# Residual stream by token tiles: normalise first, then transpose to channels

## The chip, the cores and the metric

The kernel runs on one core of a Trainium2 chip. The metric is device time of one launch in microseconds (us). The kernel before was timed three times: 2730.47, 2731.25 and 2731.49 us, median 2731.25 us. A difference of 0.2% is about 5.5 us.

## The reference

A decoder trunk of two layers over 512 tokens with 1024 channels, all in float32. A layer is three stages, and each adds its normalised result to the residual stream h:

```
f = swiglu(rms_norm(h, ffn1_pre_g), w_gate, w_up, w_down);  h = h + 0.5 * rms_norm(f, ffn1_post_g)
u = rms_norm(h, mix_pre_g);  p = u @ w_in                   # split into four branches and four gates
...
merged = g0 * y_a + g1 * y_b + g2 * y_c + g3 * y_d;         h = h + rms_norm(merged @ w_o, mix_post_g)
f = swiglu(rms_norm(h, ffn2_pre_g), w_gate, w_up, w_down);  h = h + 0.5 * rms_norm(f, ffn2_post_g)
```

`rms_norm(x, g) = x * rsqrt(mean(x * x) + 1e-6) * g`, with the mean over the 1024 channels of a token. `swiglu` has an inner width of 2816. The branches of the mixer are a gated convolution of width 3, a gated convolution of width 31 with a LayerNorm, a differential attention of 4 heads and a forgetting attention of 8 heads. The branch gates are sigmoids of 4096 further columns of `u @ w_in`.

## The kernel before, in words

**Layout.** The stream is held transposed: eight tiles `h` of 128 channels x 512 tokens. All products are taken in split float32: each factor is a high part (rounded by ScalarE in `hi_of`, L148) and a low part (the rest, by VectorE in `lo_of`, L141), and a product is three matmuls, high x high, high x low, low x high (`mm3`, L129 to L131). A stage's inputs are the eight pairs `xh`, `xl`.

**Weights.** They come as one stream of chunks of 128x1024 (512 KB), eight 128x128 blocks each, in the order in which `block` (L103) asks for them. `load` (L90) issues the DMA on SyncE's queue, rounds the high part on ScalarE (L99) and takes the low part on VectorE (L100). There are three raw buffers and five pairs of split ones, and chunks are asked for three ahead (`AHEAD`). So every 24 full-width matmuls cost ScalarE one 128x1024 cast and VectorE one 128x1024 subtraction, everywhere in the program.

**Order.** A scheduler puts the instructions of the program into one fixed queue for each engine when the kernel is built; each engine then works its queue off in order and waits at the head. PSUM has eight tiles of 128x512.

**A boundary** (`boundary`, L208) is what lies between two stages: there are seven of them, one at the start, five between stages and one at the end. The stage's input is h times a gain per channel, not yet normalised; the normalisation, a number for each token, is applied after the next stage's first products, where every result is multiplied by `rb`, a 128x512 tile that holds the 512 factors in every row (L346, L352, L409 to L415, L430 to L440, L477, L490, L558). It is made from sums of squares over channels: ScalarE squares, VectorE adds, TensorE sums over the partitions (`colsum`, L164), VectorE and GpSimdE take the power -1/2 (`rstd`, L172, L173), VectorE makes diagonal tiles (L180), TensorE spreads them (`spread`, L187). The post-norm of the stage behind is made in the same way.

So that TensorE keeps working meanwhile, the last one (FFN) or three (mixer) of the eight column groups of the down projection, and the first four products of the next stage (`outer`, L226), are taken in halves of 256 tokens: while the second half is multiplied, the norm of the first is made, and `update` (L277) goes channel tile by channel tile: multiply, add to h, scale and split, so that the first tile is there early. `CUT` tells after how many products the pieces stand.

## Time and profile before

| | |
|---|---|
| median of three runs | 2731.25 us |
| the profiled execution: its own time, its span | 2730.53 us, 2728.8 us |
| TensorE busy, matmul records | 2706.4 us (99%), 13196 |
| VectorE busy | 1617.6 us (59%) |
| ScalarE busy | 1016.6 us (37%) |
| GpSimdE busy | 55.5 us (2%) |
| DMA | 254.75 MB, mean 93 GB/s |

All times within the program are microseconds from the start of the span. Two matmuls that follow each other overlap in their records, so what a matmul costs is read from the distance of two starts, and a group's "mean ns of one" is longer than that. With VectorE and ScalarE two records overlap by some 0.08 us when the second waits for nothing (two VectorE operations of 0.42 us in 0.75 us).

### The profile page before, as it was taken

What the parts mean: (1) busy time and instruction counts of PE and PEld (TensorE: products, weight loads), DVE (VectorE), ACT (ScalarE), POOL (GpSimd) and SP (SyncE); (2) the same over time, 40 slices, a digit from 0 to 9 for tenths busy, and PEclk for the clock granted to TensorE, in tenths of its full rate; (3) what the DMA queues carried; (4) which work ended last, traced back from release to release, by engine and by line L of the source; (5) the groups of instructions that cost most, each with busy time, mean ns of one, the idle gap of its engine ahead of it and who ended that gap; (6) DMA issues with size and microseconds to landing.
All of it is one profiled execution on the core that took longest, in us unless ns stands there. A gap on an engine that the chain in (4) does not pass through costs nothing.

```text
span 2728.8 us, 33159 instructions
## 1 busy us (share of the span) xinstructions
PE 2706.4 (99%) x13196; PEld 2280.8 (84%) x13196; DVE 1617.6 (59%) x2703; ACT 1016.6 (37%) x1569; POOL 55.5 (2%) x84
## 2 busy tenths in 40 slices
PE   8999999999999999999999999999999999999998
PEld 7888898888888898888888888988888888988887
DVE  6443259988786565443364432699887865654423
ACT  4232242454553343322342322424545533432321
POOL 0000000000000000000000000000000000000000
PEclk9999999999999999999999999999999999999999
DMA  4222222222222222222222222222222222222221
GB/s 171 100 93 100 94 92 95 86 71 85 96 87 89 93 93 93 101 96 98 85 101 95 99 100 93 87 101 84 71 86 93 85 93 93 91 95 98 95 101 54
DMA packets 73786, 254.75 MB, mean 93 GB/s; under 512 B 8464, under 2 KB 10896, under 8 KB 73632
## 3 DMA queue, kind: packets, MB, share of 16 engines
q1 hardware_dynamic: 69264, 246.45, 26.4%
q10 hardware_dynamic: 4368, 6.20, 0.8%
q8 instruction: 103, 1.69, 0.3%
q14 instruction: 51, 0.42, 0.0%
HBM read 250.48 MB, written 2.13 MB: 93 GB/s over the span
## 4 chain that ended last, share of the span: by engine, by line
PE 96%; DVE 3%; ACT 1%; issue 0%; DMA 0%; POOLq 0%; DVEq 0%; ACTq 0%
PE p L129 26%; PE p L130 26%; PE p L131 26%; PE pf L130 2%; PE pf L129 2%; PE pf L131 2%; PE o L548 1%; PE pl L129 1%; PE pl L131 1%; PE pl L130 1%; PE pv L454 1%; PE pv L455 1%; PE pv L453 1%; PE pt L532 1%; PE st L187 1%; PE sc L502 1%
## 5 line engine op out<-in xcount | busy, mean ns | idle before, releaser
L99 ACT CAST wh<-raw 128x1024 fp32r<-128x1024 f32 (+1 forms) x465 | 488.5, 1051 | 1244.7 <-PE p L130 839.9
L129 PE MATMUL p<-xh,wh 128*128 128x512 f32 x2304 | 903.3, 392 | 0.0
L131 PE MATMUL p<-xh,wl 128*128 128x512 f32 x2304 | 897.5, 390 | 0.0
L130 PE MATMUL p<-xl,wh 128*128 128x512 f32 x2304 | 896.7, 389 | 0.0
L100 DVE TENSOR_TENSOR wl<-raw,wh 128x1024 fp32r<-128x1024 f32 (+1 forms) x465 | 566.9, 1220 | 390.3 <-ACT wh L99 389.6
L131 PEld LDWEIGHTS p<-xh,wl 128*128 128x128 f32 x2304 | 432.4, 188 | 91.2
L130 PEld LDWEIGHTS p<-xl,wh 128*128 128x128 f32 x2304 | 432.8, 188 | 88.4 <-issue 0.5
L129 PEld LDWEIGHTS p<-xh,wh 128*128 128x128 f32 x2304 | 432.8, 188 | 88.0 <-PE pt L532 0.5
L129 PE MATMUL p<-gh,wh 128*128 128x512 f32 x616 | 239.6, 389 | 0.0
L130 PE MATMUL p<-gl,wh 128*128 128x512 f32 x616 | 239.6, 389 | 0.0
L131 PE MATMUL p<-gh,wl 128*128 128x512 f32 x616 | 239.6, 389 | 0.0
L352 DVE TENSOR_TENSOR s<-p,rb 128x512 f32<-128x512 f32 x80 | 55.3, 691 | 238.6 <-PE p L131 238.6
L383 DVE SCALAR_TENSOR_TENSOR yc<-ba,vec,yc 128x489 f32<-128x489 f32 (+18 forms) x240 | 171.8, 729 | 1.8
L346 DVE TENSOR_TENSOR s<-p,rb 128x512 f32<-128x512 f32 x80 | 55.3, 691 | 152.6 <-PE p L131 152.5
L129 PEld LDWEIGHTS p<-gh,wh 128*128 128x128 f32 x616 | 115.6, 188 | 24.0
L131 PEld LDWEIGHTS p<-gh,wl 128*128 128x128 f32 x616 | 115.6, 188 | 24.0
L130 PEld LDWEIGHTS p<-gl,wh 128*128 128x128 f32 x616 | 115.6, 188 | 24.0
L129 PE MATMUL pf<-xh,wh 128*128 128x256 f32 (+1 forms) x352 | 104.5, 297 | 6.8 <-ACT wh L99 6.8
L130 PE MATMUL pf<-xl,wh 128*128 128x256 f32 (+1 forms) x352 | 104.3, 296 | 0.0
L131 PE MATMUL pf<-xh,wl 128*128 128x256 f32 (+1 forms) x352 | 103.8, 295 | 0.0
L522 ACT ACTIVATE e<-e,mx 128x128 f32<-128x128 f32 (+3 forms) x128 | 71.2, 557 | 53.8 <-DVE mx L520 42.6
L558 DVE TENSOR_TENSOR s<-p,rb 128x512 f32<-128x512 f32 x64 | 44.1, 689 | 66.8 <-PE p L131 66.7
(206 smaller groups left out, 3228.4 us busy)
## 6 DMA issues: line engine op xcount, KB each, us to landing
raw<-ws SPq DMA_DIRECT2D x463, 512.0 KB, 3.3
cb<-cum ACTq DMA_DIRECT2D x16, 256.0 KB, 3.6
h<-xT SPq DMA_DIRECT2D x8, 256.0 KB, 5.2
outT<-h SPq DMA_DIRECT2D x8, 128.0 KB, 1.7
outT<-h ACTq DMA_DIRECT2D x8, 128.0 KB, 1.7
raw<-ws SPq DMA_DIRECT2D x2, 256.0 KB, 4.4
cst<-consts ACTq DMA_DIRECT2D x1, 384.0 KB
s<-lamv ACTq DMA_DIRECT2D x2, 128.0 KB, 2.1
```

Source lines behind the costliest of these rows:

```text
L99: S.copy(out=wh[:, j], in_=raw[:, j])
L100: V.tensor_sub(out=wl[:, j], in0=raw[:, j], in1=wh[:, j].bitcast(F32))
L129: PE.matmul(out=out, lhsT=w[0], rhs=x[0], start=first, stop=False)
L130: PE.matmul(out=out, lhsT=w[0], rhs=x[1], start=False, stop=False)
L131: PE.matmul(out=out, lhsT=w[1], rhs=x[0], start=False, stop=last)
L187: PE.matmul(out=out[:, i * P:(i + 1) * P], lhsT=ones, rhs=dg[:, i * P:(i + 1) * P], start=True, stop=True)
L346: V.tensor_mul(out=x, in0=pg, in1=rb)
L352: V.tensor_mul(out=u, in0=pu, in1=rb)
L383: V.scalar_tensor_tensor(out=acc[:, s:], in0=y[:, :T - s], scalar=vcol(wname, l, i * 4 + j), in1=acc[:, s:], op0=ALU.mult, op1=ALU.add)
L453: PE.matmul(out=pv[t], lhsT=xh, rhs=wh, start=k == 0, stop=False)
L522: S.activation(out=e, in_=e, func=AF.Exp, scale=-1.0, bias=mx, accum_out=sums)
L558: V.tensor_mul(out=g, in0=p, in1=rb)
```

## The change: what it does

- The stream is held by tokens: four token tiles `hs[t]` of 128 tokens in two halves of 512 channels, read from `x` and written to `out` without a transposition on the host.
- The down projection (and `w_o`) is taken by token tiles (`by_tokens`): the stage's result is the stationary factor, a 128x512 strip of weights the moving one, and the result is 128 tokens x 512 channels. No half-width matmuls are left in it. The first 512 channels come first; in the second 512 the last eight strips (`HOLD`) are kept, and the four token tiles finish one after the other, each with 24 full-width matmuls.
- A token tile that is finished (`gained`, `update`, `normed`): ScalarE sums the squares of both halves with an accumulating activation, VectorE multiplies by the post-gain (a broadcast tile `gb`), `rstd_of` takes the power on GpSimdE for 128x1, VectorE adds it to h with the factor; then ScalarE squares h, a second `rstd_of`, and VectorE multiplies h by it into `u`.
- `turned` transposes u on TensorE into channel tiles, two tiles of 128x256 to a PSUM tile, and splits them with the pre-gain. It is called for the token tiles 0 and 1 ahead of `outer` for the first 256 tokens, and for 2 and 3 after six of these eight.
- The input is normalised by then, so `rb` and all multiplications with it are gone; ScalarE's activations and casts read the products from PSUM. In q and k, `hi_of` and the late `lo_of` read the product's PSUM tile. The factor 0.5 of the wide convolution goes into its weights.
- At the start, all of x is loaded, normalised and transposed ahead of the first product, which is now taken in halves too.
- The scratch pool has 59 slots in place of 62.

The core of the diff:

```diff
+HOLD = 8
...
-        sp = ctx.enter_context(tc.tile_pool(name="sp", bufs=62))
+        sp = ctx.enter_context(tc.tile_pool(name="sp", bufs=59))
...
+        def tile4(name, l, k, c):
+
+            for j in range(4):
+                block((name, l, k, c + P * j))
+            b0 = (len(order) - 4) % CB * P
+            return cur[0][:, b0:b0 + T], cur[1][:, b0:b0 + T]
+
+        def by_tokens(out, x, t, w, first, last):
+
+            r = slice(t * P, (t + 1) * P)
+            PE.matmul(out=out, lhsT=x[0][:, r], rhs=w[0], start=first, stop=False)
+            PE.matmul(out=out, lhsT=x[0][:, r], rhs=w[1], start=False, stop=False)
+            PE.matmul(out=out, lhsT=x[1][:, r], rhs=w[0], start=False, stop=last)
+
+        def rstd_of(parts, factor=1.0):
+
+            f2 = factor * factor
+            v, var, r = (np_.tile([P, 1], F32, tag=n, name=nm(n)) for n in ("nv", "nw", "nr"))
+            V.tensor_scalar(out=v, in0=parts[0], scalar1=1.0 / (D * f2), scalar2=EPS / f2, op0=ALU.mult, op1=ALU.add)
+            V.scalar_tensor_tensor(out=var, in0=parts[1], scalar=1.0 / (D * f2), in1=v, op0=ALU.mult, op1=ALU.add)
+            G.tensor_tensor(out=r, in0=var, in1=mhalf[:, 0:1], op=ALU.pow)
+            return r
+
+        def squares(src, col):
+            S.activation(out=slot(F32, "sq"), in_=src, func=AF.Square, accum_out=col)
+
         def boundary(post, pre, first):
 
 
 
 
...
+            xs, pf, blk = [], [], []
+            stat = np_.tile([P, 16], F32, tag="stat", name=nm("stat"))
+
+            def normed(t):
+
+                for c in range(2):
+                    squares(hs[t][c], stat[:, 8 + 2 * t + c:9 + 2 * t + c])
+                r = rstd_of([stat[:, 8 + 2 * t + c:9 + 2 * t + c] for c in range(2)])
+                us = [slot(F32, "u") for _ in range(2)]
+                for c in range(2):
+                    V.tensor_scalar(out=us[c], in0=hs[t][c], scalar1=r, scalar2=None, op0=ALU.mult)
+                return us
+
+            def turned(us, h):
+
+                c = HALVES[h]
+                for b in range(4):
+                    p = ps("pt")
+                    for i in range(2):
+                        k = 2 * b + i
+                        for t in range(2):
+                            o = k % 4 * P
+                            PE.transpose(out=p[:, i * H + t * P:i * H + (t + 1) * P],
+                                         in_=us[t][k // 4][:, o:o + P], identity=ident)
+                    for i in range(2):
+                        k = 2 * b + i
+                        if len(xs) <= k:
+                            xs.append((slot(F32R, "xh"), slot(F32R, "xl")))
+                        g = vcol(pre[0], pre[1], k)
+                        hi_of(xs[k][0][:, c], p[:, i * H:(i + 1) * H], g)
+                        lo_of(xs[k][1][:, c], p[:, i * H:(i + 1) * H], xs[k][0][:, c], g)
...
+            us = []
             if post is None:
...
-                    nc.sync.dma_start(out=hT[k], in_=xT[k * P:(k + 1) * P, :])
...
+                for t in range(4):
+                    for c in range(2):
+                        nc.sync.dma_start(out=hs[t][c], in_=x[t * P:(t + 1) * P, c * T:(c + 1) * T])
+                    load(t, 2 if t == 0 else 1)
+                us = [normed(t) for t in range(4)]
             else:
...
+                row, factor, name, l, ys = post
+                n = len(ys)
+                gb = gp.tile([P, D], F32, tag="gb", name=nm("gb"))
+                nc.scalar.dma_start(out=gb, in_=gains[row:row + 1, :].broadcast_to([P, D]))
+                yg = [[None, None] for _ in range(4)]
+
+                def gained(t, c, p):
+                    squares(p, stat[:, 2 * t + c:2 * t + c + 1])
+                    yg[t][c] = slot(F32, "yg")
+                    V.tensor_mul(out=yg[t][c], in0=p, in1=gb[:, c * T:(c + 1) * T])
+
+                def update(t):
+                    r = rstd_of([stat[:, 2 * t + c:2 * t + c + 1] for c in range(2)], factor)
+                    for c in range(2):
+                        V.scalar_tensor_tensor(out=hs[t][c], in0=yg[t][c], scalar=r, in1=hs[t][c],
+                                               op0=ALU.mult, op1=ALU.add)
+                        if pre is None:
+                            (nc.sync, nc.scalar)[c].dma_start(out=out[t * P:(t + 1) * P, c * T:(c + 1) * T],
+                                                              in_=hs[t][c])
+
                 settle()
...
-                last(0, nt * n, 0)
...
-                colsum(st[:, H:H + 2], acc, HALVES[0])
-                dg = diagonals(rstd(st[:, H:H + 2], D, factor))
...
-                spread(st, dg, 2)
...
-                    update(st, k, 0)
...
-                    update(st, k, 0)
...
-                    outer(0, HALVES[0])
...
-                colsum(st2[:, H:H + 2], acc, HALVES[1])
-                dg = diagonals(rstd(st2[:, H:H + 2], D, factor))
...
-                    update(st, k, 0)
...
-                spread(st2, dg, 2)
...
-                    update(st2, k, 1)
...
+                py = [ps("py") for _ in range(4)]
+                for k in range(n):
+                    w = tile4(name, l, k, 0)
+                    for t in range(4):
+                        by_tokens(py[t], ys[k], t, w, k == 0, k == n - 1)
+                    cover()
+                for t in range(4):
+                    gained(t, 0, py[t])
+                py = [ps("py") for _ in range(4)]
+                for k in range(n - HOLD):
+                    w = tile4(name, l, k, T)
+                    for t in range(4):
+                        by_tokens(py[t], ys[k], t, w, k == 0, False)
+                held = []
+                for t in range(4):
+                    for k in range(n - HOLD, n):
+                        if t == 0:
+                            held.append(tile4(name, l, k, T))
+                        by_tokens(py[t], ys[k], t, held[k - n + HOLD], k == 0, k == n - 1)
+                    gained(t, 1, py[t])
+                    update(t)
+                    if pre is not None:
+                        us.append(normed(t))
                 if pre is None:
                     return None
...
+            turned(us[0:2], 0)
+            for k in range(KD - 2):
+                outer(k, HALVES[0])
+            turned(us[2:4], 1)
+            for k in range(KD - 2, KD):
+                outer(k, HALVES[0])
             for k in range(KD):
-                acc = square_into(acc, hT[k])
+                outer(k, HALVES[1])
             pf.append(group(first[4], xs))
...
             pf.append(group(first[5], xs))
...
-            spread(st, box[1], NQ)
...
-            rb = slot(F32, "rb")
-            S.copy(out=rb, in_=st)
-            return xs, rc, rb, pf
+            return xs, pf
...
             def gate(pg):
                 x = slot()
-                V.tensor_mul(out=x, in0=pg, in1=rb)
-                S.activation(out=x, in_=x, func=AF.Silu)
+                S.activation(out=x, in_=pg, func=AF.Silu)
                 return x
 
             def up(pu, x):
                 u = slot()
-                V.tensor_mul(out=u, in0=pu, in1=rb)
-                V.tensor_mul(out=u, in0=u, in1=x)
+                V.tensor_mul(out=u, in0=pu, in1=x)
                 gs.append(split(u, s="g"))
...
             def b_in(j, pa, pg):
                 a, g = slot(F32, "ba"), slot()
-                V.tensor_mul(out=g, in0=pg, in1=rb)
-                S.activation(out=g, in_=g, func=AF.Tanh, scale=0.5)
-                V.scalar_tensor_tensor(out=a, in0=pa, scalar=0.5, in1=rb, op0=ALU.mult, op1=ALU.mult)
+                S.activation(out=g, in_=pg, func=AF.Tanh, scale=0.5)
+                V.scalar_tensor_tensor(out=a, in0=g, scalar=1.0, in1=pa, op0=ALU.add, op1=ALU.mult)
                 acc = slot(F32, "yc")
 
                 def rest():
-                    V.scalar_tensor_tensor(out=a, in0=g, scalar=1.0, in1=a, op0=ALU.add, op1=ALU.mult)
...
             def q_of(c0):
 
 
-                q = slot()
-                V.scalar_tensor_tensor(out=q, in0=proj(c0), scalar=-0.125, in1=rb, op0=ALU.mult, op1=ALU.mult)
+                q = proj(c0)
                 hi, lo = [slot(F32R, "qh"), slot(F32R, "qh")], qlo[nq[0] % 2]
                 nq[0] += 1
                 for m in range(2):
-                    hi_of(hi[m][LANES[m]], q[LANES[m]])
+                    hi_of(hi[m][LANES[m]], q[LANES[m]], -0.125)
                 for m in range(2):
-                    hi_of(hi[m][LANES[1 - m]], q[LANES[m]])
-                late.extend(lambda m=m: lo_of(lo[m][LANES[m]], q[LANES[m]], hi[m][LANES[m]]) for m in range(2))
+                    hi_of(hi[m][LANES[1 - m]], q[LANES[m]], -0.125)
+                late.extend(lambda m=m: lo_of(lo[m][LANES[m]], q[LANES[m]], hi[m][LANES[m]], -0.125) for m in range(2))
                 return hi, lo
 
             def k_of(c0):
 
-                k = slot()
-                V.tensor_mul(out=k, in0=proj(c0), in1=rb)
+                k = proj(c0)
```

**The order at a boundary.** VectorE's queue at the first boundary (FFN to mixer), before, from the point where the second half of the stream is updated: the norm of these 256 tokens is known, and each channel tile is multiplied (`fg`), added to `h` and split (`xl`) in turn.

```order
L279 TENSOR_TENSOR fg_1799<-st_2645,fg_1799 128x256
L279 TENSOR_TENSOR fg_1800<-st_2645,fg_1800 128x256
L280 TENSOR_TENSOR h_78<-h_78,fg_1799 128x256
L145 SCALAR_TENSOR_TENSOR xl_2551<-h_77,vec,xh_2550 128x256
L280 TENSOR_TENSOR h_79<-h_79,fg_1800 128x256
L145 SCALAR_TENSOR_TENSOR xl_2556<-h_78,vec,xh_2555 128x256
```

An `xl` stands right behind the tile of h that it needs; this interleaving by channel tiles is gone.

The same queue now, from token tile 2's `u` to the first low part of the next stage's input (line numbers here and below are those of the changed kernel; `wl` is the low part of a chunk of weights, `py_2283` is the last token tile's product, `h_89` and `h_90` are its two halves of the stream, `nv`, `nw` and `nr` the steps of `rstd_of`):

```order
L250 TENSOR_SCALAR u_2664<-h_87,nr_2660 128x512
L250 TENSOR_SCALAR u_2665<-h_88,nr_2660 128x512
L299 TENSOR_TENSOR yg_2694<-py_2283,gb_1928 128x512
L228 SCALAR_TENSOR_TENSOR nw_2697<-stat_1927,nv_2696 128x1
L304 SCALAR_TENSOR_TENSOR h_89<-yg_2278,nr_2698,h_89 128x512
L304 SCALAR_TENSOR_TENSOR h_90<-yg_2694,nr_2698,h_90 128x512
L101 TENSOR_TENSOR wl_2806<-raw_2804,wh_2805 128x1024
L227 TENSOR_SCALAR nv_2708<-stat_1927 128x1
L228 SCALAR_TENSOR_TENSOR nw_2709<-stat_1927,nv_2708 128x1
L250 TENSOR_SCALAR u_2714<-h_89,nr_2710 128x512
L250 TENSOR_SCALAR u_2715<-h_90,nr_2710 128x512
L146 SCALAR_TENSOR_TENSOR xl_2724<-pt_2718,vec,xh_2723 128x256
```

All of the last token tile's work, its update and its norm, stands ahead of the first low part of the first 256 tokens, which needs none of it (`pt_2718` holds transposed tiles of the token tiles 0 and 1).

ScalarE's queue now at the same place, to the first high parts:

```order
L100 CAST wh_2775<-raw_2774 128x1024
L233 ACTIVATE sq_2692,stat_1927<-py_2283 128x512
L100 CAST wh_2805<-raw_2804 128x1024
L293 DMA gb_7700<-gains 128x1024
L233 ACTIVATE sq_2704,stat_1927<-h_89 128x512
L233 ACTIVATE sq_2706,stat_1927<-h_90 128x512
L153 ACTIVATE xh_2723<-pt_2718,vec 128x256
L153 ACTIVATE xh_2727<-pt_2718,vec 128x256
```

Here too the first `xh` stands behind the squares of both halves of the last token tile.

**The order at the start.** ScalarE's queue before (`h_77` is the first channel tile, `wh_114` the first weights):

```order
L152 ACT_TABLE_LOAD
L152 ACTIVATE xh_110<-h_77,vec 128x512
L99 CAST wh_114<-raw_113 128x512 x2
L152 ACTIVATE xh_140<-h_78,vec 128x512
L152 ACTIVATE xh_157<-h_79,vec 128x512
```

and now, from the third of its five chunks of weights on:

```order
L100 CAST wh_140<-raw_139 128x1024
L233 ACTIVATE sq_183,stat_117<-h_88 128x512
L100 CAST wh_148<-raw_147 128x1024
L233 ACTIVATE sq_195,stat_117<-h_89 128x512
L233 ACTIVATE sq_197,stat_117<-h_90 128x512
L100 CAST wh_495<-raw_494 128x1024
L153 ACTIVATE xh_214<-pt_209,vec 128x256
L153 ACTIVATE xh_218<-pt_209,vec 128x256
```

The first `xh` stood second in the queue; it now stands behind the squares of all of x and behind the casts of five chunks.

More of the change, by code (lines that the diff above doesn't have):

```diff
@@ L53, with build @@
 NCOLS = DEPTH * VL
-def build(tc, ws, xT, vecs, wdf, lamv, fb, consts, outT):
+def build(tc, ws, x, vecs, gains, wdf, lamv, fb, consts, out):
     nc = tc.nc
@@ L318, in boundary @@
                 if pre is None:
                     return None
-                pend.pop()()
-                for k in range(KD):
-                    outer(k, HALVES[1])
-            acc = None
+            turned(us[0:2], 0)
[4 more added lines that the diff above has]
+                outer(k, HALVES[0])
             for k in range(KD):
-                acc = square_into(acc, hT[k])
+                outer(k, HALVES[1])
@@ L362, in ffn @@
             settle()
-            groups = [[(f"ffn{n}_w_down", l, k, m * P) for k in range(KF)] for m in range(KD)]
-            return f"ffn{n}_post_g", l, 0.5, groups, gs, 1
+            return 3 * l + 2 * n - 2, 0.5, f"ffn{n}_w_down", l, gs
         def cols(l, c0):
@@ L446, in values @@
                 for k in range(KD):
-                    for j in range(4):
-                        block(("w_in", l, k, c0 + P * j))
-                    b0 = (len(order) - 4) % CB * P
-                    wh, wl = cur[0][:, b0:b0 + T], cur[1][:, b0:b0 + T]
+                    w = tile4("w_in", l, k, c0)
                     for t in range(NQ):
-                        xh, xl = xs[k][0][:, t * P:(t + 1) * P], xs[k][1][:, t * P:(t + 1) * P]
-                        PE.matmul(out=pv[t], lhsT=xh, rhs=wh, start=k == 0, stop=False)
-                        PE.matmul(out=pv[t], lhsT=xh, rhs=wl, start=False, stop=False)
-                        PE.matmul(out=pv[t], lhsT=xl, rhs=wh, start=False, stop=k == KD - 1)
+                        by_tokens(pv[t], xs[k], t, w, k == 0, k == KD - 1)
                     if k % 2 == 1:
@@ L557, in gate @@
                 g = slot()
[L558 to L559 removed]
+                S.activation(out=g, in_=p, func=AF.Tanh, scale=0.5)
                 gates[br, m] = g
@@ L583, in mixer @@
             pace[0] = PACE[1]
-            vc = [split(p, scale=rc[:, t:t + 1], s="v") for t, p in enumerate(values(OFF_CV))]
+            vc = [split(p, s="v") for p in values(OFF_CV)]
             q, k = q_of(OFF_CQ), k_of(OFF_CK)
@@ L657, in mixer @@
             nc.scalar.dma_start(out=cum, in_=e[0:8])
-            vd = [paired(p, rc[:, t:t + 1]) for t, p in enumerate(values(OFF_DV))]
+            vd = [paired(p) for p in values(OFF_DV)]
             def b_norm():
@@ L746, in mixer @@
             settle()
-            return "mix_post_g", l, 1.0, [[("w_o", l, k, m * P) for k in range(KD)] for m in range(KD)], merged, 3
+            return 3 * l + 1, 1.0, "w_o", l, merged
         vec = cp.tile([P, NCOLS], F32, name="vec")
         nc.scalar.dma_start(out=vec, in_=vecs)
-        hT = [cp.tile([P, T], F32, name=f"h{k}") for k in range(KD)]
+        hs = [[cp.tile([P, T], F32, name=f"h{t}{c}") for c in range(2)] for t in range(NQ)]
         cst = cp.tile([P, 2 * P + T], F32, name="cst")
@@ L780, in vcol @@
             return vec[:, c:c + 1]
+        for l in range(DEPTH):
+            c = l * VL + _VOFF["b_conv_w"]
+            V.tensor_scalar(out=vec[:, c:c + 124], in0=vec[:, c:c + 124], scalar1=0.5, scalar2=None, op0=ALU.mult)
         post = None
@@ L807, in _pack @@
     consts = np.concatenate([np.eye(P, dtype=np.float32), mask, dist], 1)
-    xT = np.ascontiguousarray(np.asarray(inputs["x"])[0].T)
-    return {"xT": xT, "vecs": vecs, "wdf": wdf, "lamv": lamv, "fb": fb, "consts": consts}
+    gains = np.ascontiguousarray(np.stack([np.asarray(inputs[n])[l] for l in range(DEPTH)
+                                           for n in ("ffn1_post_g", "mix_post_g", "ffn2_post_g")]))
+    x = np.ascontiguousarray(np.asarray(inputs["x"])[0])
+    return {"x": x, "vecs": vecs, "gains": gains, "wdf": wdf, "lamv": lamv, "fb": fb, "consts": consts}
 def _stream(inputs, order):
@@ L828 @@
     aps = {n: nc.dram_tensor(n, list(s), F32, kind="ExternalInput").ap() for n, s in shapes.items()}
-    outT = nc.dram_tensor("outT", [D, T], F32, kind="ExternalOutput").ap()
+    out = nc.dram_tensor("out", [T, D], F32, kind="ExternalOutput").ap()
     with tile.TileContext(nc) as tc:
-        order = build(tc, outT=outT, **aps)
+        order = build(tc, out=out, **aps)
     assert len(order) == NBLK
@@ L834 @@
     r = run_bass_kernel_spmd(nc, [arrays], core_ids=[0])
-    return np.ascontiguousarray(r.results[0]["outT"].T)[None]
+    return np.ascontiguousarray(r.results[0]["out"])[None]
```

99 lines of the change are left out of this document (11 added, 88 removed).

## The prediction

> **What bounds the kernel now.** First the page's busy times and TensorE's waits, all of them:
>
> ```profile
> PE 2706.4 (99%) x13196; PEld 2280.8 (84%) x13196; DVE 1617.6 (59%) x2703; ACT 1016.6 (37%) x1569; POOL 55.5 (2%) x84
> ...
> PE pf L129 <- ACT wh L99: 6.8, 1, 6.8
> PE pt L532 <- DVE e L601: 3.1, 8, 0.8
> PE pt L532 <- DVE e L706: 1.7, 3, 0.7
> PE st L187 <- DVE dg L180: 1.4, 1, 1.4
> PE st L164 <- DVE sq L272: 0.9, 1, 0.9
> ```
>
> TensorE is never idle between 6.8 us and the end but for 4.8 us in the mixers' transpositions (L532) and 2.3 us in the last boundary. Less work on VectorE or ScalarE is therefore worth 4.8 us at most; the time can otherwise change only by TensorE's own work, by waits that are new, and by start and end. A table by stages (start, first FFN, the boundary behind it, first mixer, end; columns are the length, then busy time and count of PE, PEld, DVE, ACT, POOL, then clock and DMA) tells how full the engines are there:
>
> ```profile
> 0.00:31.00 31.00, 24.16 (x96) 19.67 (x97) 22.64 (x36) 18.72 (x27) 0.20 (x4) 1.00 0.72 259
> ...
> 355.00:396.00 41.00, 41.00 (x342) 40.87 (x341) 30.87 (x69) 20.10 (x36) 1.40 (x2) 1.00 0.23 78
> 396.00:978.00 582.00, 579.70 (x2739) 480.77 (x2738) 444.34 (x821) 250.34 (x435) 21.44 (x32) 1.00 0.27 89
> ...
> 2699.90:2728.80 28.90, 18.20 (x149) 17.71 (x147) 13.68 (x41) 2.67 (x6) 1.39 (x2) 0.88 0.22 73
> ```
>
> At the boundary VectorE is busy for 31 of 41 us and TensorE all the time: the halves cover the norm completely. That cover is what the change rebuilds.
>
> **TensorE's own work.** What a matmul costs is the distance of starts (start, duration, then the instruction):
>
> ```profile
> 349.78 0.39 PE L129 MATMUL p<-gh,wh 128*128 128x512 f32 x1
> ...
> 350.23 0.39 PE L131 MATMUL p<-gh,wl 128*128 128x512 f32 x1
> ...
> 355.22 0.28 PE L129 MATMUL pl<-gh,wh 128*128 128x256 f32 x1
> ...
> 364.45 0.28 PE L131 MATMUL pl<-gh,wl 128*128 128x256 f32 x1
> 364.57 0.50 PE L164 MATMUL st<-ones,sq 128*128 128x1 f32 x4
> 364.94 0.36 PE L129 MATMUL pl<-gh,wh 128*128 128x256 f32 x1
> ...
> 36.63 0.79 PE col L164 x8
> 43.02 0.89 PE st L187 x8
> 721.69 1.09 PE pt L532 x10
> ```
>
> A 128x512 costs 0.227 us (two steps from 349.78 to 350.23); 78 of 128x256 stand between 355.22 and 364.57, 0.120 each, so that two halves cost 0.013 more than a whole. Per boundary between stages: the down projection's 132 (FFN) or 144 (mixer) halves become 66 or 72 wholes, -0.9. `col` and `st` over 512 tokens go, -1.7. The two pairs of `colsum` and `spread` over halves go (364.57 to 364.94 is 0.37 for one `colsum`; a `spread` of four records as much), -1.5. 32 transpositions come, 10 of which took 1.09: +3.5. The sum is -0.6. The token-wise products have the shape of the values' (L453 to L455), which run at the same 0.227; they are counted at no change.
>
> **The boundary's new wait.** The last token tile is finished with the last matmul of the projection (time 0). From there TensorE has only the 16 transpositions of tiles 0 and 1, 1.75 us, since the next matmul needs `xh` and `xl`, and in both queues these stand behind the last token tile's update and norm (the two fences on the boundary's order). Durations, from groups by shape (count, busy us, mean ns of one):
>
> ```profile
> L99 ACT CAST wh<-raw 128x1024 fp32r<-128x1024 f32 x463 | 487.3, 1053 | 1244.7 <-PE p L130 839.9 <-issue 313.4 <-PE pv L455 28.0
> L202 ACT ACTIVATE sq<-h 128x512 f32<-128x512 f32 x48 | 28.7, 617 | 0.0
> L522 ACT ACTIVATION_READ_ACCUMULATOR e<-e,mx 128x1 f32 x128 | 23.9, 187 | 0.0
> L100 DVE TENSOR_TENSOR wl<-raw,wh 128x1024 fp32r<-128x1024 f32 x463 | 565.6, 1222 | 390.3 <-ACT wh L99 389.6
> L346 DVE TENSOR_TENSOR s<-p,rb 128x512 f32<-128x512 f32 x80 | 55.3, 691 | 152.6 <-PE p L131 152.5
> L601 DVE SCALAR_TENSOR_TENSOR e<-e,sums,e 128x512 f32<-128x512 f32 x8 | 6.0, 752 | 0.3
> L600 DVE TENSOR_SCALAR e<-e,sums 128x512 f32<-128x512 f32 x8 | 3.9, 487 | 0.3
> L172 DVE TENSOR_SCALAR var<-st 128x2 f32<-128x2 f32 x12 | 1.9, 156 | 6.0 <-PE st L164 6.0
> L173 POOL TENSOR_TENSOR r<-var,mhalf 128x2 f32<-128x2 f32 x12 | 8.4, 697 | 1699.8 <-DVE var L172 1699.8
> L145 DVE SCALAR_TENSOR_TENSOR v<-pv,r,v 128x256 fp32r<-128x256 f32 x16 | 6.5, 477 | 3.9 <-ACT v L152 3.9
> ```
>
> The power for 128x1 does not occur: 128x4 and 128x2 take 1.48 and 0.70, so half of the latter, 0.35, is taken; from nothing to 0.70 would move a boundary by 0.7 either way, there being two in the chain. A squaring with its accumulator is 0.62 + 0.19 = 0.80. A record that follows another of its engine costs 0.08 less than its mean.
>
> VectorE is the slower queue, so I lay it out from time 0. Token tile 2 has been finished 5.4 us (24 x 0.227) earlier, and its two updates of h are just done. What is left: the rest of a subtraction `wl`, 0.5; three small steps, 0.35; `wl` of the next chunk with a short wait for its cast, 1.35; two `u`, 0.82; `yg` from PSUM, 0.61; `nw` and the power, 0.67; two `h`, 1.34; another `wl`, 1.14; `nv`, `nw` and the second power (ScalarE's squares of both halves, 1.6, lie beside the `wl`), 0.83; two `u`, 0.82; the first `xl`, 0.48. Sum 8.9 us. The first `xh` comes at about 6.5, behind the squares. So TensorE is idle from 1.75 to 6.5, runs four matmuls, and waits until 8.9: a stall of 8.9 - 1.75 - 0.48 = 6.7 us. Behind that, ScalarE and VectorE deliver a channel tile in about 0.75 us, for which TensorE needs 12 x 0.120 = 1.44: no further wait. The `u` of tiles 2 and 3 are ready before TensorE asks for them, six tiles later. The held strips need four chunks in 5.4 us, 4 x 1.22 = 4.9 on VectorE, and are split ahead; I take no wait, 1 us at worst. Bounds of the stall: 5 (the `wl` all before time 0) to 9. Per boundary 6.7 - 0.6, with five of them **+30.5**.
>
> **Start.** Rows of the first 16 us:
>
> ```profile
> 6.84 0.80 PE L129 MATMUL pf<-xh,wh 128*128 128x512 f32 x1 [6.84 <-ACT wh L99]
> 8.55 0.36 SPq L98 DMA_DIRECT2D raw<-ws  x1
> 9.17 0.63 PE L131 MATMUL pf<-xh,wl 128*128 128x512 f32 x1
> 9.60 0.63 PE L129 MATMUL pf<-xh,wh 128*128 128x512 f32 x1
> 11.30 0.60 PE L130 MATMUL pf<-xl,wh 128*128 128x512 f32 x1
> 13.35 0.39 PE L129 MATMUL pf<-xh,wh 128*128 128x512 f32 x1
> 15.32 1.05 ACT L99 CAST wh<-raw 128x1024 fp32r<-128x1024 f32 x1 [0.34 <-DMA raw<-ws]
> ```
>
> The chunk issued at 8.55 was there at 15.32: loading limits. The first `xh` now stands behind the fifth chunk's cast (the fences on the start). That chunk is issued once the second has left its raw buffer, at 13 to 13.5, and lands 3.3 (median) to 6.8 us later; with cast, `xh`, and the `wl` and `xl` on VectorE the first channel tile is complete at 21 to 24, I take 22, in place of 7.9 (the third of the first matmuls, two slow steps behind 6.84): +14.1. The product in halves adds 192 x 0.120 - 96 x 0.227 = 1.3, the second 16 transpositions 1.75, `col` and `st` go with 1.7. **+15.5**, between 13 and 19.
>
> **End.** Before, behind the last product:
>
> ```profile
> 2716.82 0.38 ACT L271 ACTIVATE sq<-pl 128x256 f32<-128x256 f32 x1 [8.05 <-PE pl L131]
> ...
> 2725.16 0.75 DVE L280 TENSOR_TENSOR h<-h,fg 128x256 f32<-128x256 f32 x2
> ```
>
> From 2716.8 to the end 12.0 us. Now square 0.8, `yg` 0.6, `nw` and power 0.6, two `h` 1.4, and 2.8 from the last `h` to the end as before (2725.9 to 2728.8): 6.2, so -5.8. The halves (0.9) and the other pair of sums (0.7) go too: **-7.5**, between -6 and -9.5.
>
> **In the stages.** Without `rb`, VectorE loses some 390 operations; TensorE's idle time there, 4.8 us, could go. Against it, q and k now keep their PSUM tile until the late low parts have read it, and the scheduler has laid the transpositions of the mixers' fourth head 2 to 6 us nearer to their weights. I take **0**, from -5 to +12.
>
> **The clock.** TensorE starts slow: 0.43 us from 9.17 to 9.60, 0.227 from 13.35 on. The slow time runs from 6.84 to 11.3, 4.5 us, and loses about half of it, 2.1. At the end the granted clock falls (the last column but two of these windows):
>
> ```profile
> 2720.00:2723.00 3.00, 0.45 (x4) 0.26 (x3) 2.73 (x9) 0.00 (x0) 0.00 (x0) 0.82 0.31 104
> 2723.00:2725.00 2.00, 0.00 (x0) 0.00 (x0) 2.00 (x7) 0.00 (x0) 0.00 (x0) 0.50 0.51 171
> ```
>
> 0.82 over three microseconds is a fall to 0.5 at about 2721.9, 5 us behind the last dense products (2716.8), though four short matmuls lie in the first of the windows. The new gap is like it: 7 us with four matmuls. So I expect the clock to fall at each of the five boundaries and to cost what it costs at the start; from 0 to 2.1 each, I take the whole, **+10**. The Trainium skill ("TensorE: Matmul & The Clock Gate", "What's actually happening") has the clock halved after an idle window of about 3.4 us and released after as long a busy one; the two rows agree with it, and it would make the term 5 x 1.7 = 8.5.
>
> Sum: 30.5 + 15.5 - 7.5 + 0 + 10 = +48.5. The profiled execution lasted 2730.53, 1.7 more than its span, and with that stays 2779.0; the median of the runs lies 0.7 above that execution: **2780**.
>
> **Rivals.** *The clock stays*: the term of 10 falls away, **2770**; for it speaks that the transpositions stand in the gap and may count as work, against it the short matmuls at the end, which did not help. *The mixers stall*: VectorE's attention chain is the only one that already delays TensorE there (L601, L706); 6 us more in each mixer, for the PSUM tiles that q and k hold, gives **2792**; against it, TensorE 99.6% busy there before, with 138 us in which VectorE is idle. *The chain is hidden* (the other side): if the first `xl` came within the transpositions, as it does not depend on the last token tile, the five stalls and the clock fall away, 5 x -0.6 + 15.5 - 7.5 = +5, and with the mixers' 4.8 us gained **2732**, no change that can be told. It decides at 1.75 us behind the last product; the order speaks against it, as VectorE works its queue in order and 8 us stand ahead.
>
> **How the numbers follow.** The forecast 52%, its own range 2770 to 2788 (stall 6 to 8, start 13 to 19, clock 1 to 2.1 each); the clock stays 20%; the mixers 15%; the chain hidden 8%; else 5%. To hold 8 in 10: 2764 to 2792. Runs tell 0.2%, 5.5 us, from no change; so faster 0.03, same 0.05, slower 0.92.
>
> **What would show it.** TensorE's waits should name `pf` behind ACT `xh` and DVE `xl`, five times each, 4 to 5.5 and 1 to 2 us, and at the start `xh` at 20 to 22 us. The granted clock should fall to 0.5 at each boundary, and twelve half matmuls behind the stall take 2.9 us rather than 1.44; if not, it stayed. From the end of the first `outer` to that of the next, an FFN and its boundary (31.0 to 396.0, 365 us), should be 373 long. The prediction is wrong if the waits at `pf` are below 2 us, if `py` waits for `wh` by more than 1 us, or if the mixers' `pt` waits grow beyond 5 us each.

## The result and the profile after

The changed kernel takes **2796.03 us**, the median of four runs (2795.15 to 2796.86), beside 2730.86 for the kernel before: 1.0239 times as long (95% interval 1.0221 to 1.0256), 65.2 us more. The forecast was 2780 with a range of 2764 to 2792: the direction was right, the size too small by 16 us, a quarter of what happened, and the range missed by 4.

The busy times and TensorE's waits of the kernel after:

```profile
PE 2720.7 (97%) x12884; PEld 2280.1 (82%) x12884; DVE 1392.6 (50%) x2287; ACT 980.0 (35%) x1607; POOL 75.7 (3%) x114
```

```profile
PE pf L130 <- ACT xh L153: 30.3, 6, 5.6
PE pt L262 <- DVE u L250: 14.8, 2, 11.9
PE pt L529 <- DVE e L597: 11.5, 4, 3.6
PE pf L131 <- DVE xl L146: 9.6, 6, 1.7
```

VectorE has lost 225 us of work (1617.6 to 1392.6) and TensorE 312 matmul records, and the kernel is slower: the waits have grown from 14 us to 66. Four rows stand there. `pf` behind `xh` and `xl` is the boundary (five times, and once at the start). `pt` behind `u` is the start. `pt` behind `e` (L597) is in the mixers, where 4.8 us stood before. What the list does not show is the clock.

A table by stages, each from the first `p` behind one boundary's halves to the next such `p` (starts of matmuls in the trace; us):

| stage | before | after | difference |
|---|---|---|---|
| start, to the first `p` | 31.0 | 49.9 | +18.9 |
| FFN and boundary | 365.0 | 374.7 | +9.7 |
| mixer and boundary | 624.7 | 638.9 | +14.2 |
| FFN and boundary | 365.0 | 373.2 | +8.2 |
| FFN and boundary | 365.0 | 374.3 | +9.3 |
| mixer and boundary | 625.0 | 638.6 | +13.6 |
| last FFN, end | 353.1 | 344.3 | -8.8 |

All boundaries lose alike, and each mixer loses some 5 us beyond its boundary.

**The boundary.** The first one, from the timeline (start, duration, engine; in brackets the idle time before and its releaser):

```profile
386.99 0.40 PE L221 MATMUL py<-wh,gl 128*128 128x512 f32 x1
...
387.23 1.91 PE L262 MATMUL pt<-cst,u 128*128 128x128 f32 x16
...
388.24 1.22 DVE L101 TENSOR_TENSOR wl<-raw,wh 128x1024 fp32r<-128x1024 f32 x1
388.39 1.48 POOL L229 TENSOR_TENSOR nr<-nw,mhalf 128x1 f32<-128x1 f32 x1 [4.23 <-DVE nw L228]
...
389.90 0.88 DVE L250 TENSOR_SCALAR u<-h,nr 128x512 f32<-128x512 f32 x2 [0.44 <-POOL nr L229]
...
391.60 0.55 POOL L229 TENSOR_TENSOR nr<-nw,mhalf 128x1 f32<-128x1 f32 x1 [1.73 <-DVE nw L228]
392.18 1.42 DVE L304 SCALAR_TENSOR_TENSOR h<-yg,nr,h 128x512 f32<-128x512 f32 x2 [0.73 <-POOL nr L229]
...
394.26 0.46 ACT L153 ACTIVATE xh<-pt,vec 128x256 fp32r<-128x256 f32 x1
...
394.77 0.79 PE L130 MATMUL pf<-xh,wh 128*128 128x256 f32 x2 [5.63 <-ACT xh L153]
...
396.74 0.47 DVE L146 SCALAR_TENSOR_TENSOR xl<-pt,vec,xh 128x256 fp32r<-128x256 f32 x1
...
397.26 0.58 PE L131 MATMUL pf<-xl,wh 128*128 128x256 f32 x1 [1.70 <-DVE xl L146]
```

TensorE finishes the last product at 387.2, transposes until 389, and waits 5.6 us for `xh` and 1.6 to 1.7 for `xl`, while four `u`, two `h` and three powers (`nr`) of the last two token tiles go ahead of the first `xl`, and the two `h` and their squares ahead of the first `xh`. The clock beside it (window, length, PE, PEld, DVE, ACT, POOL, then granted clock and DMA):

```profile
389.00:394.70 5.70, 0.14 (x2) 0.00 (x0) 4.53 (x9) 2.78 (x6) 1.42 (x2) 0.87 0.85 304
394.70:397.20 2.50, 0.79 (x2) 0.50 (x2) 1.66 (x6) 0.01 (x1) 1.33 (x3) 0.50 0.58 192
397.20:400.00 2.80, 2.74 (x13) 2.74 (x14) 1.71 (x5) 1.68 (x4) 0.00 (x0) 0.50 0.11 40
400.00:403.00 3.00, 3.00 (x16) 3.00 (x16) 1.41 (x4) 2.32 (x4) 0.00 (x0) 0.50 0.12 31
403.00:404.00 1.00, 1.00 (x8) 1.00 (x8) 0.38 (x4) 0.28 (x1) 0.00 (x0) 0.77 0.12 39
```

TensorE is busy again from 397.26, yet the clock stays at 0.5 until 403.46 (0.77 over the last microsecond). Over these 6.2 us a half product takes 0.213 in place of 0.120.

**The mixers.** The fourth head of the first mixer:

```profile
673.27 0.69 DVE L517 CUSTOM_DVE_ANT_0 e<-sc,bias 128x512 f32<-128x512 f32 x1
...
676.21 0.49 PE L529 MATMUL pt<-cst,e 128*128 128x128 f32 x3
676.74 0.69 DVE L517 CUSTOM_DVE_ANT_0 e<-sc,bias 128x512 f32<-128x512 f32 x1 [2.77 <-PE pt L529]
...
678.87 0.55 PE L529 MATMUL pt<-cst,e 128*128 128x128 f32 x3 [2.17 <-DVE e L597]
...
679.87 1.38 DVE L146 SCALAR_TENSOR_TENSOR qlo<-p,qh 64x512 fp32r<-64x512 f32 x2
...
682.20 0.75 DVE L597 SCALAR_TENSOR_TENSOR e<-e,sums,e 128x512 f32<-128x512 f32 x1
...
683.01 1.12 PE L529 MATMUL pt<-cst,e 128*128 128x128 f32 x4 [3.59 <-DVE e L597]
```

The odd row is 676.74. VectorE adds the bias to scores that have been in PSUM since 668, and waits for a *transposition* of the same head, one of the consumers of such rows. In the built program the tile that this row writes (`e1`, row 3) has the address of `e0`, row 1: the transposition at 676.21 is the last reader of that buffer. So the pool of common buffers is empty at this place, and a producer waits for a consumer further down. Behind it the last softmax row comes 3.6 us late. The clock falls in these waits too:

```profile
679.00:683.00 4.00, 0.42 (x3) 0.18 (x3) 3.85 (x8) 0.50 (x1) 0.62 (x1) 0.62 0.38 131
683.00:685.00 2.00, 1.99 (x7) 1.80 (x8) 1.97 (x3) 1.03 (x3) 0.68 (x1) 0.50 0.00 0
```

### The profile page after: what moved, and what is told of

It reads as the page before. It is cut to its first block, busy times and chain, and to the rows that moved or that the text cites. A ratio compares the mean times of both kernels' runs of the same rounds, so it can differ in the third digit from the quotient of the medians.

```text
span 2793.9 us, 32240 instructions
## 1 busy us (share of the span) xinstructions
PE 2720.7 (97%) x12884; PEld 2280.1 (82%) x12884; DVE 1392.6 (50%) x2287; ACT 980.0 (35%) x1607; POOL 75.7 (3%) x114
## 4 chain that ended last, share of the span: by engine, by line
PE 95%; DVE 3%; POOL 1%; issue 1%; DMA 0%; ACT 0%; ACTq 0%; POOLq 0%; DVEq 0%; SPq 0%
PE p L130 21%; PE p L132 21%; PE p L131 21%; PE py L220 6%; PE py L221 6%; PE py L219 6%; PE pf L131 2%; PE pf L132 2%; PE pf L130 2%; PE o L545 1%; PE pv L219 1%; PE pv L221 1%; PE pv L220 1%; PE pt L529 1%; POOL nr L229 1%; PE sc L499 1%
## 5 line engine op out<-in xcount | busy, mean ns | idle before, releaser
L221 PE MATMUL py<-wh,gl 128*128 128x512 f32 x704 | 273.9, 389 | 0.0
L219 PE MATMUL py<-wh,gh 128*128 128x512 f32 x704 | 273.9, 389 | 0.0
L220 PE MATMUL py<-wl,gh 128*128 128x512 f32 x704 | 273.9, 389 | 0.0
L392 DVE SCALAR_TENSOR_TENSOR yc<-ba,vec,yc 128x501 f32<-128x501 f32 (+17 forms) x240 | 169.7, 729 | 2.4
L219 PEld LDWEIGHTS py<-wh,gh 128*128 128x128 f32 x704 | 132.1, 188 | 27.6
L220 PEld LDWEIGHTS py<-wl,gh 128*128 128x128 f32 x704 | 132.1, 188 | 27.4
L221 PEld LDWEIGHTS py<-wh,gl 128*128 128x128 f32 x704 | 132.1, 188 | 27.3
L130 PE MATMUL pf<-xh,wh 128*128 128x256 f32 x384 | 115.0, 304 | 30.3 <-ACT xh L153 30.3
L131 PE MATMUL pf<-xl,wh 128*128 128x256 f32 x384 | 115.9, 302 | 9.6 <-DVE xl L146 9.6
L132 PE MATMUL pf<-xh,wl 128*128 128x256 f32 x384 | 114.7, 299 | 0.0
```

The costliest lines, as they stand in the source:

```text
L130: PE.matmul(out=out, lhsT=w[0], rhs=x[0], start=first, stop=False)
L131: PE.matmul(out=out, lhsT=w[0], rhs=x[1], start=False, stop=False)
L132: PE.matmul(out=out, lhsT=w[1], rhs=x[0], start=False, stop=last)
L219: PE.matmul(out=out, lhsT=x[0][:, r], rhs=w[0], start=first, stop=False)
L220: PE.matmul(out=out, lhsT=x[0][:, r], rhs=w[1], start=False, stop=False)
L221: PE.matmul(out=out, lhsT=x[1][:, r], rhs=w[0], start=False, stop=last)
```

## Experiments

The kernels below compute everything that the changed kernel (or, in one, the kernel before) computes; two of them add products into a PSUM tile that nothing reads. All stages are those of the table above (us):

| kernel | start | FFN | mixer | FFN | FFN | mixer | end |
|---|---|---|---|---|---|---|---|
| before | 31.0 | 365.0 | 624.7 | 365.0 | 365.0 | 625.0 | 353.1 |
| after | 49.9 | 374.7 | 638.9 | 373.2 | 374.3 | 638.6 | 344.3 |
| 1 first pair early | 48.9 | 366.9 | 631.7 | 366.9 | 366.8 | 631.7 | 344.4 |
| 2 pool of 61 | 48.6 | 373.2 | 630.9 | 374.4 | 373.4 | 630.9 | 344.6 |
| 3 before, pool of 61 | 30.9 | 364.9 | 631.5 | 365.0 | 365.0 | 631.6 | 353.6 |
| 4 gap filled | 50.4 | 372.1 | 636.6 | 372.0 | 372.1 | 637.5 | 344.4 |
| 5 start | 41.0 | 373.8 | 640.5 | 373.5 | 374.4 | 638.7 | 344.3 |
| 6 three orders and the pool | 40.0 | 365.1 | 622.2 | 365.5 | 365.3 | 622.0 | 344.6 |
| 7 five gaps | 50.4 | 373.5 | 640.1 | 373.1 | 374.4 | 636.6 | 344.4 |
| 8 HOLD = 4 | 50.2 | 382.0 | 645.9 | 381.7 | 382.1 | 645.9 | 344.3 |

### 1. The first pair of token tiles early

```diff
                     if pre is not None:
                         us.append(normed(t))
+                    if t == 2 and pre is not None:
+                        turned(us[0:2], 0)
                 if pre is None:
                     return None
-            turned(us[0:2], 0)
+            if post is None:
+                turned(us[0:2], 0)
```

> The changed kernel, but the transpositions and splits of tokens 0 to 255 stand in the program before the third token tile's successor: behind the norm of token tile 2 and ahead of the last products of token tile 3. Theory (the stall at the boundary is queue order: the first xh and xl stand behind the last tile's update and norm): TensorE's waits for xh (5.6 us) and xl (1.7 us) at the five boundaries fall below 1 us each, the clock does not fall there, and each first product in halves no longer loses its 2 to 3 us; 5 x 9 us go, 2796 becomes about 2752 (2748 to 2760), an FFN stage with its boundary 365 to 367 long. Rival (the split itself, or the second pair's u, is late whatever the order): the wait turns up a little later in the same product, 2780 to 2796.

Measured: 2760.78 (2759.13 to 2761.51), 35 us less than the changed kernel and just above the range expected. TensorE's waits at and behind the boundary:

```profile
PE pt L262 <- DVE u L250: 7.4, 11, 2.9
PE pf L131 <- DVE xl L146: 2.4, 4, 1.5
...
PE pf L130 <- DVE xl L146: 2.0, 5, 0.4
```

The 5.6 us are gone, and the granted clock is 1.00 all along the first boundary; each stage is 6.3 to 7.8 us shorter. That is the queue order, as the theory has it. But 2 us per FFN stage stay: `pt` now waits for `u`, 0.2 to 0.7 us at a time, and `pf` for `xl`, up to 0.4 (the 2.9 and 1.5 of these rows are at the start). The last token tile's norm has been pushed behind eight splits, and the small part of the rival that was true is this.

### 2 and 3. The pool of buffers

The gains go into two tiles of the common pool, which makes room for 61 buffers in place of 59:

```diff
-        sp = ctx.enter_context(tc.tile_pool(name="sp", bufs=59))
+        sp = ctx.enter_context(tc.tile_pool(name="sp", bufs=61))
-                gb = gp.tile([P, D], F32, tag="gb", name=nm("gb"))
-                nc.scalar.dma_start(out=gb, in_=gains[row:row + 1, :].broadcast_to([P, D]))
+                gb = [slot(F32, "gb") for _ in range(2)]
+                for c in range(2):
+                    nc.scalar.dma_start(out=gb[c], in_=gains[row:row + 1, c * T:(c + 1) * T].broadcast_to([P, T]))
```

> The changed kernel with the broadcast gains in two tiles of the common pool, which gets 61 in place of 59 buffers; nothing else. Theory (the new waits of the mixers' transpositions come from the pool: in the fourth head the last exponentials wait until a transposition has read the buffer that they are given): the waits of 2.2 and 3.6 us in each mixer and the fall of the clock behind them go, 5 us per mixer, 2796 becomes about 2786 (2783 to 2789). Rival (q and k, which keep their PSUM tile until the late low parts have read it): no change, 2796.

Measured: 2778.17 (2777.17 to 2779.85), 18 us less, where some 10 were expected: the cause is the one named, its price was set too low. In the kernel before, with one number changed:

```diff
-        sp = ctx.enter_context(tc.tile_pool(name="sp", bufs=62))
+        sp = ctx.enter_context(tc.tile_pool(name="sp", bufs=61))
```

> The kernel before with 61 buffers in the common pool in place of 62, nothing else. Theory of the pool: the same waits turn up in the kernel before, in the fourth head of both mixers, 2 to 4 us each, with a fall of the clock: 4 to 7 us per mixer, 2731 becomes 2739 to 2746. Rival (PSUM held by q and k, which this kernel does not do): 2731, no change.

Measured: 2745.61 (2744.29 to 2746.37), 1.0055 of the kernel before (1.0040 to 1.0070), 15 us more, in the range expected. The waits of TensorE in the mixers of the first of the two:

```profile
PE pt L529 <- DVE e L597: 0.3, 2, 0.2
```

and the timeline of the second, the fourth head again:

```profile
650.15 0.49 PE L532 MATMUL pt<-cst,e 128*128 128x128 f32 x3
650.68 0.69 DVE L520 CUSTOM_DVE_ANT_0 e<-sc,bias 128x512 f32<-128x512 f32 x1 [2.52 <-PE pt L532]
...
652.81 0.62 PE L532 MATMUL pt<-cst,e 128*128 128x128 f32 x3 [2.17 <-DVE e L601]
...
657.01 1.12 PE L532 MATMUL pt<-cst,e 128*128 128x128 f32 x4 [3.58 <-DVE e L601]
```

It is the same row, waiting for the same transposition, with the same 2.17 and 3.6 us behind it, in a kernel without any of the change's edits. The kernel before has not one buffer to spare: the 62nd is worth 15 us. That settles it against the rival, since this kernel holds no q and k in PSUM. In the changed kernel the shortage costs 8.0 and 7.7 us per mixer: waits of 2.2 and 3.6, and the clock that falls in them. Without it the mixers are shorter than before the change (by 2.5 and 3.0 in experiment 6), as TensorE no longer waits there for `e`, 2.4 each.

### 4. The gap filled with work

```diff
             turned(us[0:2], 0)
+            if post is not None:
+                fill = ps("fill")
+                for i in range(28):
+                    PE.matmul(out=fill, lhsT=ys[0][0][:, :P], rhs=ys[1][0], start=True, stop=True)
             for k in range(KD - 2):
                 outer(k, HALVES[0])
```

> The changed kernel with 28 products of 128x512 (28 x 0.227 = 6.4 us) into an unused PSUM tile between the transpositions of tokens 0 to 255 and the first product in halves, at each of the five boundaries; they lie in the time in which TensorE waits. Theory (the clock term of the prediction: TensorE's idle time lets the clock fall, and the products behind it run at half speed for 5 to 6 us): the granted clock stays at 1.0 there, the products behind start at 0.12 us a step, 5 x 2.1 to 2.8 us go: 2796 becomes 2782 to 2786, with the stall itself as long as before. Rival (the halves run slow for another reason, such as waiting for their xh and xl): 2796 or more.

Measured: 2786.35 (2785.75 to 2787.47), 9.7 us less, at the upper end of what was expected, though TensorE does 6.4 us more at each boundary and waits for `xl` as before. The stages lose 1.1 to 2.6 us each. The fall of the clock has its own price, and it is about the one predicted.

### 5. The start

```diff
-                for t in range(4):
-                    for c in range(2):
-                        nc.sync.dma_start(out=hs[t][c], in_=x[t * P:(t + 1) * P, c * T:(c + 1) * T])
-                    load(t, 2 if t == 0 else 1)
-                us = [normed(t) for t in range(4)]
+                with tc.manual_schedule(engines={mybir.EngineType.DVE, mybir.EngineType.Activation}):
+                    fetch(0)
+                    fetch(1)
+                    us = [normed(0), normed(1)]
+                    load(0, 2)
+                    fetch(2)
+                    fetch(3)
+                    turned(us[0:2], 0, (0, 1))
+                    load(1)
+                    turned(us[0:2], 0, (2,))
+                    us += [normed(2)]
+                    load(2)
+                    turned(us[0:2], 0, (3,))
+                    us += [normed(3)]
+                    load(3)
```

(`fetch(t)` is the two transfers of a token tile; `turned` takes a list of its four groups of two channel tiles.)

> The changed kernel with another order at the start only: x's first two token tiles are fetched and squared before the first chunk's casts, the transpositions and first splits follow at once, and the other chunks' casts and the other two norms stand between the later splits. Theory (start: the first xh stands behind five chunks' casts and all squares): TensorE's first product in halves begins at 11 to 13 us in place of 20.9, its first complete channel tile comes at 12 to 14 in place of 24, and the first p begins at 41 to 44 in place of 49.9 (the products then wait for chunks a little); 6 to 9 us go: 2787 to 2790. Rival (the fetch of x and of the chunks sets the start, whatever the order): 2793 to 2797.

Measured: 2787.33 (2785.89 to 2787.95), 8.7 us less; the first product in halves begins at 13.1 and the first `p` at 41.0. Half of the start's loss was order. The other half stays with this order, and no other was run; what speaks for a cost of the change itself is that the kernel before needed one channel tile of `x` and one chunk to begin, and this one needs two whole token tiles, their norm and a transposition.

### 6. The orders and the pool together

Edits 2 and 5, and at the boundary the four groups of the first pair spread:

```diff
+PLAN = {(2, 0): (0,), (2, 2): (1,), (3, 1): (2,), (4, 0): (3,)}
...
+                    turn(t, 0)
                     update(t)
+                    turn(t, 1)
                     if pre is not None:
                         us.append(normed(t))
+                    turn(t, 2)
                 if pre is None:
                     return None
+                turn(4, 0)
```

(`turn(t, i)` calls `turned(us[0:2], 0, PLAN[t, i])` where the plan has an entry.)

> Three orders and the pool together: the start of the run before, the pool of 61 buffers with the gains in it, and at the boundary the four groups of two channel tiles of tokens 0 to 255 spread: the first ahead of token tile 2's update, the second behind its norm, the third behind token tile 3's update, the fourth behind its norm. Theory (the loss of the change is these three orders and nothing in its arithmetic): from 2796, start -8, mixers -16 as the pool alone gave, boundaries -9 each, 2727 (2720 to 2734), an FFN stage with its boundary 365 us as before the change; TensorE waits nowhere above 1.5 us behind the start. Rival (the second pair of tiles is late in any order, as VectorE is full there, 1.9 us each as in the first order tried): 2736 to 2740.

Measured: 2726.86 (2726.36 to 2727.89), 0.9988 of the kernel before (0.9979 to 0.9997), 3.5 us faster. TensorE's waits, all of them:

```profile
PE pt L263 <- DVE u L251: 12.0, 9, 7.8
PE pt L552 <- DVE e L620: 0.2, 1, 0.2
```

7.8 of the 12.0 us lie ahead of TensorE's first instruction. The FFN stages are back at 365, the mixers 2.5 and 3.0 below before, the end 8.5 below; only the start is worse, by 9.0. What the change computes costs nothing outside the start; its loss there was order and buffers. What it gains, when these are mended, is 0.1%, which is less than the 0.2% that the prediction counts as no change.

### 7. Gaps of five lengths

The filler of experiment 4 with 6, 10, 14, 18 and 22 products at the five boundaries.

> The changed kernel with 6, 10, 14, 18 and 22 products of 128x512 into an unused PSUM tile between the transpositions and the first product in halves, at the five boundaries in turn (they leave TensorE idle for about 4.3, 3.4, 2.5, 1.6 and 0.7 us, then four short products and the wait for xl of 1.7). Theory (the clock falls after a time without work): where 4.3 and 3.4 us are left it falls and the stage is about 374 or 639 long as without them, from 2.5 down it does not, and the stage is 2 to 3 us shorter. Rival (any gap does it, or the wait for xl behind it counts as well): all five as before; 2796, against 2788 to 2790.

Measured: 2794.19 (one run); FFN, mixer, FFN, FFN, mixer differ from the changed kernel by -1.2, +1.1, -0.1, +0.1 and -2.0. Only the last is the gain expected, and the lengths alone would not show it, as stages that experiment 5 leaves as they are differ by up to 1.6 in its trace. What tells is the clock, in these rows with 18 (the first three) and 22 products:

```profile
1780.00:1784.00 4.00, 1.06 (x6) 0.54 (x4) 3.16 (x8) 1.75 (x5) 1.33 (x3) 0.94 0.70 194
1784.00:1790.00 6.00, 5.66 (x26) 5.66 (x27) 3.39 (x8) 3.93 (x8) 0.00 (x0) 0.50 0.15 57
1790.00:1791.00 1.00, 1.00 (x9) 1.00 (x8) 0.28 (x3) 0.34 (x1) 0.00 (x0) 0.82 0.25 82
2420.00:2424.00 4.00, 1.75 (x10) 1.12 (x9) 2.69 (x7) 1.61 (x7) 0.55 (x1) 1.00 0.61 204
2424.00:2430.00 6.00, 6.00 (x52) 6.00 (x51) 3.11 (x7) 2.55 (x7) 0.00 (x0) 1.00 0.03 8
```

With 18 no single gap is longer than 1.8 us, and the clock falls all the same, 0.94 over four microseconds in which TensorE worked for 1.06. With 22 it worked for 1.75 of them, and the clock stayed. The expectation took the longest gap as what counts, and that was wrong: the rival, that the wait for `xl` counts too, was right for 14 and 18 products. What does count is worked out at the end.

### 8. HOLD = 4

```diff
-HOLD = 8
+HOLD = 4
```

> The changed kernel with HOLD = 4: the last products of a token tile are 12 in place of 24, so token tile 2 is finished 2.7 us before the last one, and not 5.4. Theory (the stall is the queue of VectorE and ScalarE at the last product, the sum of 8.9 us): more of token tile 2's update and norm is left at time 0, and the stall grows by at least the 2.7 us, up to 7 us with the transpositions that wait for their u: 5 x 2.7 to 7, 2796 becomes 2810 to 2830. Rival (the stall is one fixed chain behind the last product of the last tile alone): 2796.

Measured: 2833.33 (2832.43 to 2834.28), 37 us more than with 8, some 7.5 per boundary, just above the upper bound given:

```profile
PE pf L130 <- ACT xh L153: 43.7, 6, 9.1
PE pt L262 <- DVE u L250: 34.5, 7, 11.7
```

The stall is the backlog of the two queues at the last product, not one chain behind it: leave the token tile before it 2.7 us less, and the wait for `xh` grows from 5.6 to between 8.0 and 9.1, while the transpositions begin to wait 3.8 to 4.1 for their `u`.

## Why the prediction was partly right and missed its range

Its terms, and what the runs make of them (us). The measured boundary is 7.2 to 7.3 of wait, less TensorE's own work; the clock is the slow time with dense work at each boundary (6.2, 5.1, 3.1, 5.2 and 4.7 us) times 0.44, which is 1 - 0.120 / 0.213; the stages' term is what is left of the mixers. `col` and `st` of a boundary lie in the stage behind it, so 1.7 goes from the start to the first stage and from the last boundary to the end.

| term | predicted | measured |
|---|---|---|
| five boundaries | +30.5 | +34.8 |
| start | +15.5 | +17.2 |
| end | -7.5 | -7.1 |
| in the stages | 0 | +9.6 |
| clock | +10 | +10.6 |
| sum | +48.5 | +65.1 |

The sum is the difference of the two spans, 2793.9 and 2728.8. (The end's own terms add up to -7.4, not -7.5.)

**The bound** was right: VectorE's 225 us were worth nothing but the mixers' 4.8, and what moved the time were new waits, the start and the end.

**The boundary's wait** was right in place, cause and form: `pf` behind `xh` (4 to 5.5 predicted, 5.6 measured) and `xl` (1 to 2, and 1.6 to 1.7), 7.3 in place of 6.7. VectorE's 8.9 us were 10.0, 397.2 less 387.2, and its mis-sized part is mostly the power. 0.35 was half of a 128x2; a 128x1 takes 0.55. Two were counted in the chain, and a third, of token tile 2's norm, was taken as done: it is the first behind the last product, and takes 1.48. VectorE stands idle for 0.44, 0.73 and 0.73 us before the three operations that need a power. The 1.48 that the prediction quotes for a 128x4 was a mixture (below). No run changes the power alone. TensorE's own work came out at -0.3 per boundary in place of -0.6 (first stage: 9.7 less 7.3 of wait and 2.7 of clock).

**The clock** was right, 10.6 for 10, and experiment 4 shows it alone. The flat 2.1 hid a spread of 1.3 to 2.7, so that the total is closer than its parts.

**Start and end** were inside their bounds. The first `xh` came at 20.9; the first complete channel tile came at 24.0, not 22, since on VectorE `u` and another `wl` stood ahead of `xl`:

```profile
20.90 1.22 PE L130 MATMUL pf<-xh,wh 128*128 128x256 f32 x4 [2.20 <-ACT xh L153]
21.15 0.88 DVE L250 TENSOR_SCALAR u<-h,nr 128x512 f32<-128x512 f32 x2 [0.66 <-POOL nr L229]
21.95 1.22 DVE L101 TENSOR_TENSOR wl<-raw,wh 128x1024 fp32r<-128x1024 f32 x1
23.08 0.48 DVE L146 SCALAR_TENSOR_TENSOR xl<-pt,vec,xh 128x256 fp32r<-128x256 f32 x1
...
24.00 0.42 PE L132 MATMUL pf<-xh,wl 128*128 128x256 f32 x1
```

**The step that failed is "In the stages ... I take 0, from -5 to +12".** It saw the order's sign, the fourth head's transpositions nearer to their weights, and gave it no price; it looked for a cause in PSUM, and passed over the line of the diff that takes three buffers from the common pool. The rival *the mixers stall* had the place (L601, now L597) and nearly the size, 6 us each against 4.8, and the wrong cause: experiments 2 and 3 put it on the pool. Its argument against itself, that TensorE was 99.6% busy there and VectorE idle for 138 us, says nothing about buffers: a full pool does not show as a busy engine. The +9.6, of the 16.6 us by which the sum is short, is itself a difference: the shortage of buffers costs 8.0 and 7.7 (experiment 2), and without it the mixers are some 3 us shorter each than before. The prediction's own sign of being wrong, `pt` waits of more than 5 us in each mixer, came true: 2.17 and 3.59 are 5.8. Had the term been +10, the sum would have been 2790; the rest of the miss is mostly the boundaries, 4.3.

**The rival on the other side**, the chain hidden, was wrong for this order and right as a possibility: experiment 1 hides the chain, and experiment 6 does so with the start and the pool mended.

## What to carry to other kernels

A change that rebuilds a cover has to be read for three things at once: what stands ahead of the first operand in each in-order queue at the moment the cover ends, how many buffers the pool has left where it is fullest, and whether enough work stands beside the gap to keep the clock. A line that lowers a pool by a few buffers needs a price like any other: look for the place where the most tiles live at once, and ask which producer would wait for which consumer there. When a change loses everywhere alike, mend the order before judging the idea.

## What the runs showed of the hardware

**The power on GpSimd waits for VectorE's two-input operation.** All 48 powers of 128x1 in the changed kernel (duration least, median, most, in ns):

```profile
L229 POOL TENSOR_TENSOR nr<-nw,mhalf x48: 550/551/1492, 10.8 to 2788.7; 128x1 f32<-128x1 f32 x48
```

43 take 0.55 us. The five of 1.48 to 1.49 are the first behind the last product of each boundary, and each begins 0.15 us after a `wl` (a subtraction of two SBUF tiles) and ends 0.4 behind it, as in the boundary's timeline above. In experiment 6 five powers beside a `wl` take 1.43 to 1.44, and five beside an `xl`, which reads PSUM and one SBUF tile, 0.55. In the kernel before, the 128x4 powers take 1.85 beside a `wl`, 1.38 beside a `qlo` and 1.01 else: their mean of 1.48 was no price of the operation. The Trainium skill ("SBUF — State Buffer", "SBUF: two separate sides") has VectorE and GpSimd share a pair of ports that an operation with two SBUF inputs holds for its whole length against a GpSimd operation that reads SBUF; the traces agree with it.

**The clock's fall and return are not set by one gap.** It fell where no gap was longer than 1.8 us but two of them enclosed 0.7 us of short products, and did not where the gaps were 0.6 and 1.6. It returned between 3.1 and 6.2 us after the products ran densely again. All ten traces show why: within each, the changes of the clock lie whole multiples of 3.413 us apart (in the changed kernel at 393.22, 403.46, 679.94 and 686.77, which is 3, 81 and 2 steps). Cut along that grid, every stretch at full clock that ends ahead of the last product and had at most 1.40 us of TensorE busy, by its records, ended in a fall, and every one with at least 1.53 did not. At half clock, every stretch with at least 2.82 us brought the full clock back, and none with up to 2.79 did. In experiment 7 the poorest stretch holds 0.04, 0.74, 1.12, 0.93 and 1.79 us, so only the fifth keeps the clock. The Trainium skill ("TensorE: Matmul & The Clock Gate", "What's actually happening") has a window of about 3.4 us that runs freely and does not start with the work; the traces agree with it. What a fall costs thus depends on where the dense products begin in the grid: at the third boundary they fill 3.06 us of the stretch to 1413.81, and the clock is back after 3.1 us; at the first they begin at 397.26, fill too little of the stretch to 400.05, and need the next one as well, to 403.46.
